# An earlier, two-part position bias and strictly alternating partial matmuls in the first block of a two-block kernel

## The chip, the cores and the metric

One Trainium2 chip, one NeuronCore of it. The metric is the device time of one execution, in microseconds (us). The kernel before was timed three times: 1125.5, 1128.43 and 1130.07 us, so its median is 1128.43 us. A further execution was profiled; its own time is 1129.25 us.

## The reference

Two transformer blocks run one after the other on a sequence of 256 tokens of width 1024, all in float32. The change lies in the first one, whose mixer has two attention branches of eight heads each and needs this, cut to what matters here:

```python
h = rmsnorm(x, norm_mix); proj = h @ w_in        # split into q_a, k_a, ..., kv_b, g_b, g_br
# branch A: an index scores every key, the best 64 of them are attended to
score = sum_h wi * relu(qi_h @ k_i.T)            # 8 index heads of width 32, causal
logits = q_a @ k_a.T * scale + table_a[t5_bucket(t - s)]
# branch B: compressed blocks, selected blocks, window; all three use the other 8 columns of the table
kc_cmp = compress_blocks(kc)                     # gelu(blk @ w1) @ w2 on blocks of 32 tokens, stride 16
logit_c = q_b @ kc_cmp.T * scale + table_b[t5_bucket(t - cmp_end)]
logit_s = q_b @ k_s.T * scale + table_b[t5_bucket(t - s)]
logit_w = q_b @ k_w.T * scale + table_b[t5_bucket(t - s)]
x = x + (sigmoid(gate_a) * (o_a @ w_branch_a) + sigmoid(gate_b) * (o_b @ w_branch_b)) @ w_out
```

The bias depends on the distance t - s alone: a table of 32 buckets by 16 heads (`rel_bias`) gives one value for each head and distance.

## The kernel before, in words

All weights stream from memory in units of 128 x 1024 float32 values (512 KB, two K-tiles of 512 columns). SyncE's queue issues the loads into four `raw` buffers (line 246); ScalarE rounds a unit to `hi` (line 262) and VectorE subtracts to get `lo` (line 263), each into four buffers; TensorE multiplies hi and lo with the hi and lo parts of the activations, three matmuls for each product (lines 349, 351, 352 where the result has features on partitions, 305 to 307 where it has tokens there). A raw buffer is free again when `lo` is made, so the stream runs a fixed number of units ahead of TensorE.

Small work is woven into these matrix products: `later` puts functions into a list, and each K-tile of a product takes one from it. Within this, a scheduler with a model of its own sets the order of TensorE's, VectorE's and ScalarE's queues; GpSimd's (POOL) and SyncE's queues keep the order in which the program is written. Every engine works its queue strictly in order.

In `block1_mix` the order of the products is: the token-wise columns (chunk 4 of `w_in`), queries and keys of the index (chunk 0), keys and values (chunk 1), `qb` (chunk 3), `qa` (chunk 2), then four chunks of gates, into which the attention itself is woven. What the change touches:

- `bias_job` (line 587). A matmul of `rb` with a one-hot matrix (line 590) gives the bias of 16 heads for 384 distances; VectorE adds the causal mask (`tv`, 592); GpSimd writes it sixteen times, once for each row of a group of 16 queries, to device memory (`tvd`, 595) and reads it back shifted by one element from row to row in eight DMAs (597), 16 queries with 16 heads each, into `BT` (128 x 16 heads x 256). Then GpSimd clears `cmpB` and copies every sixteenth column of heads 8 to 15 into it (600 to 602). The job is queued ahead of chunk 3.
- The memsets of `kcT`, `VB`, `gek`, `gev` (741, 743, 773), which stand behind that job in GpSimd's queue.
- The loads of the compression weights `w1k`, `w1v` (1 MB each, 703) and of `csk`, `csv`, and the copies of keys and values `kpk`, `kpv` (717, 718) from which `blkk`, `blkv` are added up (725).
- `index` (657): eight score matmuls for each 128 queries; each uses 32 rows of the 128 x 128 array (`32*128`), four such row groups in turn. `cmp1` (746): 16 matmuls into four column groups. `qk` (845): query-key products of the attention; each uses 64 rows, head pairs lie in the lower and the upper half. In the source these loops alternate between the groups already; the scheduler may place them in another order.
- `bm` (837, GpSimd) adds the index's mask to heads 0 to 7 of `BT` for branch A; the softmax (866) of branch B reads heads 8 to 15. The order of branches is selected, window, A.

Of the kernel before, what the change touches and what calls it, by code (L numbers as in the profile page):

```python
# [9 lines left out]
F32 = mybir.dt.float32  # L10
# [13 lines left out]
NEG = -1.0e30  # L24
# [185 lines left out]
class Prog:  # L210
# [343 lines left out]
    def block1_mix(self, x0, x):  # L554
        tc, nc, ap, g = self.tc, self.nc, self.ap, self.g
        with ExitStack() as es, ExitStack() as rs_:
# [3 lines left out]
            cp = pool("b1c", 1)  # L560
# [19 lines left out]
            BT = cp.tile([128, 16, 256], F32, name="BT")  # L580
# [7 lines left out]
            def bias_job():  # L588
# [37 lines left out]
            def small_done(t, ps):  # L626
                nc.scalar.activation(tms[:, t, :], ps, AF.Copy, scale=r0[:, t:t + 1])
                if t:
                    nc.scalar.activation(gb, tms[:, :, 328:352], AF.Tanh, scale=0.5)
                    nc.gpsimd.tensor_scalar(gb, gb, 0.5, 0.5, op0=ALU.mult, op1=ALU.add)  # L630
                    nc.gpsimd.dma_start(caus, ap["c1"][:, tot - 256:])
                    nc.gpsimd.dma_start(rest, ap["c1"][0:32, 128:896])
                    nc.gpsimd.dma_start(rb, ap["rel_bias"])
            stats()
# [16 lines left out]
            self.gemm_feat(W_IN1, 0, *xT, d0)  # L651

# [4 lines left out]
            def index(t, hps):  # L657
# [3 lines left out]
                for a in range(2):  # L661
                    for hp, ps in zip(hps, pss):
                        pr = slice(32 * hp, 32 * hp + 32)
                        nc.tensor.matmul(ps[:, a, :n], qi[pr, a, t * 128:t * 128 + 128], ki[pr, :n], start=True,
                                         stop=True)
# [35 lines left out]
            for nm in "kv":  # L701
                w1 = mp.tile([128, 16, 128], F32, name="w1" + nm)
                nc.gpsimd.dma_start(w1, ap["cmp_w1_" + nm])
                cs = mp.tile([128, 80], F32, name="cs" + nm)
                nc.gpsimd.dma_start(cs, ap["cmp_s_" + nm])
                cw.append((w1, cs))
            blks = []

            def d1(i, ps):
                nc.vector.tensor_tensor(kv[:, 2 * i:2 * i + 2, :], ps, bc2, op=ALU.mult)  # L710
                if i:
                    return
                for i, nm in enumerate("kv"):
# [5 lines left out]

                    blk = mp.tile([128, 16, 32], F32, name="blk" + nm)  # L720
                    nc.gpsimd.memset(blk[:, :, 30:32], 0.0)
                    for gr in range(2):
                        v = bass.AP(tensor=kp.tensor, offset=kp.offset + 256 * gr,
                                    ap=[list(kp.ap[0]), [2, 16], [16, 15]])
                        nc.gpsimd.tensor_tensor(blk[:, :, 15 * gr:15 * gr + 15], v,
                                                cw[i][1][:, 0:16].unsqueeze(2).to_broadcast([128, 16, 15]),
                                                op=ALU.add)
                    blks.append(blk)
# [7 lines left out]
            self.later(bias_job)  # L736
# [3 lines left out]
            kcT = cp.tile([128, 2, 16], F32, name="kcT")  # L740
            nc.gpsimd.memset(kcT, 0.0)
            VB = cp.tile([128, 2, 4, 64], F32, name="VB")
            nc.gpsimd.memset(VB, 0.0)
            cps = {}

            def cmp1(i):
# [3 lines left out]
                for l4 in range(4):  # L750
                    for q in range(4):
                        l = 4 * l4 + q
                        nc.tensor.matmul(ps[32 * q:32 * q + 32, :128], blks[i][:, l, :], cw[i][0][:, l, :],
# [882 lines left out]
```

## Time and profile before

| | |
|---|---|
| time, median of three runs | 1128.43 us (1125.5 to 1130.07) |
| the profiled execution's own time | 1129.25 us |
| its span, first to last instruction | 1127.5 us |
| TensorE busy | 1104.7 us, 98% of the span |
| VectorE, ScalarE, GpSimd busy | 762.8, 573.7, 93.3 us |
| mean granted TensorE clock | 0.993 of full speed |
| `block1_mix` | about the first 220 us |

A share of 98% says that nearly all of the time is TensorE's queue at work, so a change counts only by what it does to that queue: an instruction in it that becomes shorter, or a wait in it that goes or comes. Idle time of the other engines is read only for what it makes TensorE wait for.

### The profile page before, as it was taken

The page shows a single profiled execution, that of the slowest core. Times are in us where ns is not written, and L with a number is a line of the kernel's source. Part 1 is how long each engine was busy: PE and PEld are TensorE (multiplying, and loading weights), DVE is VectorE, ACT ScalarE, POOL GpSimd, SP SyncE. Part 2 cuts the span into 40 slices and gives each one's busy share as a digit, 9 for nine tenths or more (in the row PEclk, how much of TensorE's full clock was granted, in tenths as well). Part 3 has the DMA queues.
Part 4 walks back from the last instruction along what each step waited for, and adds up shares of the span by engine and source line. Part 5 has one row for each costly group of instructions (what it writes and reads, how often), then busy time and mean ns, then how long its engine had stood idle before and what let it go on. Part 6 is the DMA issues. An engine that isn't in the chain of part 4 may idle for free.

```text
span 1127.5 us, 17685 instructions
## 1 busy us (share of the span) xinstructions
PE 1104.7 (98%) x6852; PEld 986.4 (87%) x6852; DVE 762.8 (68%) x1230; ACT 573.7 (51%) x858; POOL 93.3 (8%) x135
## 2 busy tenths in 40 slices
PE   9998999999999999999999999999999999999997
PEld 8887899888888878888879999889999978888886
DVE  6766777677755567777458675556778777777643
ACT  6325544555544456555445336545555455655542
POOL 1411230000001010000001010001323000000000
PEclk9998999999999999999999999999999998999999
DMA  8794124655555646555556655444544565555552
GB/s 298 250 175 145 39 86 149 210 179 196 189 187 182 199 168 201 186 187 186 186 169 201 195 168 200 152 130 139 181 150 157 163 204 167 188 186 185 189 173 92
DMA packets 55908, 196.91 MB, mean 175 GB/s; under 512 B 6716, under 2 KB 6988, under 8 KB 55568
## 3 DMA queue, kind: packets, MB, share of 16 engines
q1 hardware_dynamic: 52704, 186.44, 50.2%
q0 software_dynamic: 2832, 9.21, 3.5%
q8 instruction: 54, 0.88, 0.3%
q14 instruction: 30, 0.25, 0.1%
q10 hardware_dynamic: 288, 0.14, 0.1%
HBM read 192.84 MB, written 1.44 MB: 172 GB/s over the span
## 4 chain that ended last, share of the span: by engine, by line
PE 92%; DVE 3%; DMA 3%; ACT 1%; issue 1%; POOL 0%; DVEq 0%; POOLq 0%; ACTq 0%
PE acc L368 20%; PE acc L369 10%; PE acc L305 10%; PE acc L306 9%; PE acc L307 9%; PE acc L351 8%; PE acc L349 8%; PE acc L352 8%; DMA BT<-tvd 2%; PE sm L854 2%; PE o L893 1%; DVE lo L263 1%; PE tr L880 1%; PE o L1437 1%; PE sm L1407 1%; PE tr L399 1%
## 5 line engine op out<-in xcount | busy, mean ns | idle before, releaser
L263 DVE TENSOR_TENSOR lo<-raw,hi 128x1024 fp32r<-128x1024 f32 (+2 forms) x356 | 433.3, 1219 | 264.8 <-ACT hi L262 262.4
L262 ACT ACTIVATE hi<-raw 128x1024 fp32r<-128x1024 f32 (+2 forms) x356 | 371.2, 1044 | 425.4 <-issue 120.9
L368 PE MATMUL acc<-xs,hi 128*128 128x512 f32 x960 | 340.4, 400 | 1.3 <-DVE sum L374 1.0
L369 PE MATMUL acc<-xs,lo 128*128 128x256 f32 x960 | 268.8, 281 | 0.0
L368 PEld LDWEIGHTS acc<-xs,hi 128*128 128x128 f32 x960 | 180.8, 189 | 44.8 <-DVE sum L374 1.4
L349 PE MATMUL acc<-xs,hi 128*128 128x256 f32 (+1 forms) x696 | 198.7, 288 | 0.3 <-ACT hi L262 0.3
L351 PE MATMUL acc<-xs,hi 128*128 128x256 f32 (+1 forms) x696 | 198.1, 286 | 0.0
L352 PE MATMUL acc<-xs,lo 128*128 128x256 f32 (+1 forms) x696 | 197.0, 286 | 0.1
L369 PEld LDWEIGHTS acc<-xs,lo 128*128 128x128 f32 x960 | 181.9, 189 | 0.5
L349 PEld LDWEIGHTS acc<-xs,hi 128*128 128x128 f32 (+1 forms) x696 | 132.9, 192 | 3.4 <-issue 2.4
L351 PEld LDWEIGHTS acc<-xs,hi 128*128 128x128 f32 (+1 forms) x696 | 133.5, 192 | 1.9 <-issue 1.5
L352 PEld LDWEIGHTS acc<-xs,lo 128*128 128x128 f32 (+1 forms) x696 | 132.8, 192 | 1.6 <-issue 1.0
L305 PE MATMUL acc<-hi,hT 128*128 128x512 f32 x304 | 117.9, 390 | 1.0 <-DVE x L1069 1.0
L306 PE MATMUL acc<-lo,hT 128*128 128x512 f32 x304 | 118.5, 390 | 0.0
L307 PE MATMUL acc<-hi,hT 128*128 128x512 f32 x304 | 118.0, 389 | 0.0
L305 PEld LDWEIGHTS acc<-hi,hT 128*128 128x128 f32 x304 | 57.1, 188 | 13.3 <-DVE x L1069 1.5
L307 PEld LDWEIGHTS acc<-hi,hT 128*128 128x128 f32 x304 | 57.1, 188 | 12.0
L306 PEld LDWEIGHTS acc<-lo,hT 128*128 128x128 f32 x304 | 57.1, 188 | 11.5
L305 PE MATMUL acc<-hi,xs 128*128 128x386 f32 (+1 forms) x128 | 47.7, 375 | 1.6 <-DVE f L1160 1.5
L306 PE MATMUL acc<-lo,xs 128*128 128x386 f32 (+1 forms) x128 | 48.0, 375 | 0.0
L307 PE MATMUL acc<-hi,xs 128*128 128x386 f32 (+1 forms) x128 | 46.8, 370 | 0.0
L374 DVE TENSOR_TENSOR sum<-acc,sum 128x512 f32<-128x512 f32 x60 | 41.0, 684 | 0.0
(430 smaller groups left out, 1344.5 us busy)
## 6 DMA issues: line engine op xcount, KB each, us to landing
raw<-in_w_in SPq DMA_DIRECT2D x100, 512.0 KB, 3.5
raw<-in_ffn_w_gate SPq DMA_DIRECT2D x44, 512.0 KB, 3.5
raw<-in_ffn_w_up SPq DMA_DIRECT2D x44, 512.0 KB, 3.4
raw<-in_ffn_w_down SPq DMA_DIRECT2D x44, 512.0 KB, 3.4
raw<-in_w_mlp_in SPq DMA_DIRECT2D x32, 512.0 KB, 3.4
raw<-in_w_mlp_out SPq DMA_DIRECT2D x32, 512.0 KB, 3.2
raw<-in_w_out SPq DMA_DIRECT2D x16, 512.0 KB, 3.5
raw<-in_w_in SPq DMA_DIRECT2D x16, 386.0 KB, 3.1
```

Of the source, the lines that this page charges most:

```text
L262: nc.scalar.activation(hi[:, :n * w], raw[:, :n * w], AF.Copy)
L263: nc.vector.tensor_tensor(lo[:, :n * w], raw[:, :n * w], hi[:, :n * w], op=ALU.subtract)
L305: nc.tensor.matmul(ps[t][:, :w], xh[:, k, sl], hi, start=(k == 0), stop=False)
L306: nc.tensor.matmul(ps[t][:, :w], xh[:, k, sl], lo, start=False, stop=False)
L307: self.last_mm = nc.tensor.matmul(ps[t][:, :w], xl[:, k, sl], hi, start=False, stop=last)
L349: nc.tensor.matmul(o, hi[:, fs], xh[:, k, :], start=(k == 0 and f % 2 == 0), stop=False, skip_group_check=True)
L351: nc.tensor.matmul(o, hi[:, fs], xl[:, k, :], start=False, stop=False, skip_group_check=True)
L352: nc.tensor.matmul(o, lo[:, fs], xh[:, k, :], start=False, stop=last, skip_group_check=True)
L368: nc.tensor.matmul(ps[:, f, :, :], hi[:, fs], x.both[:, k, :, :], start=(k == 0), stop=False)
L369: nc.tensor.matmul(ps[:, f, 0, :], lo[:, fs], x.hi[:, k, :], start=False, stop=last)
L374: nc.vector.tensor_tensor(s, ps[:, :, 0, :], s, op=ALU.add)
L854: nc.tensor.matmul(ps[:, i, :], q[pr:pr + 64, U["fts"][i], t * 128:t * 128 + 128], kk, start=True, stop=True)
```

## The change

`bias_job` becomes two parts. `bias_table` (matmul, mask, write to memory) is called right behind chunk 0. `bias_rows(g)` reads back eight heads in eight DMAs; it is called with g = 1 (heads 8 to 15) ahead of chunk 1 and with g = 0 behind the first chunk of gates. `BT` becomes two tiles. The memsets stand ahead of the reads, the loads of `w1k`, `csk`, `csv` behind them; `w1v` is loaded behind the copies for `kpk` and `kpv`. The copies into `cmpB` follow `blkv`. `rest` and `rb` are loaded ahead of `caus`. A new helper, `in_turn`, forces each matmul of `index`, `cmp1` and `qk` behind the one written before it in TensorE's queue; it adds no instruction.

```diff
+    def in_turn(self, fs):
+        last = None
+        for f in fs:
+            with ExitStack() as es:
+                if last is not None:
+                    es.enter_context(self.tc.issue_after(last.ins))
+                last = f()
...
-            BT = cp.tile([128, 16, 256], F32, name="BT")
+            BT = [cp.tile([128, 8, 256], F32, name="BT%d" % g) for g in range(2)]
...
-            def bias_job():
+            def bias_table():
                 ps = self.psm()
                 nc.tensor.matmul(ps[:16, :384], rb, onehot, start=True, stop=True)
                 tv = bp.tile([16, 384], F32, name="tv")
                 nc.vector.tensor_tensor(tv, ps[:16, :384], neg, op=ALU.add)
-                tvd = self.dp.tile([16, 16, 384], F32, name="tvd")
+                tvd = box["tvd"] = self.dp.tile([16, 16, 384], F32, name="tvd")
                 nc.gpsimd.dma_start(tvd.rearrange("c h u -> h c u"), tv.unsqueeze(1).to_broadcast([16, 16, 384]))
+
+            def bias_rows(g):
+                tvd = box["tvd"]
                 for i in range(8):
-                    nc.gpsimd.dma_start(BT[16 * i:16 * i + 16, :, :],
-                                        bass.AP(tensor=tvd.tensor, offset=tvd.offset + 127 - 16 * i,
-                                                ap=[[16 * 384 - 1, 16], [384, 16], [1, 256]]))
-                nc.gpsimd.memset(cmpB, NEG)
-                nc.gpsimd.tensor_copy(cmpB[:, 1, :, 0:15], BT[:, 8:16, 31:256:16])
-                nc.gpsimd.tensor_copy(cmpB[:, 0, :, 0:7], BT[:, 8:16, 159:256:16])
+                    nc.gpsimd.dma_start(BT[g][16 * i:16 * i + 16, :, :],
+                                        bass.AP(tensor=tvd.tensor, offset=tvd.offset + 8 * 384 * g + 127 - 16 * i,
+                                                ap=[[16 * 384 - 1, 16], [384, 8], [1, 256]]))
...
             self.gemm_feat(W_IN1, 0, *xT, d0)
+            bias_table()
...
-                for a in range(2):
-                    for hp, ps in zip(hps, pss):
...
+                self.in_turn([lambda a=a, z=z: score(a, *z) for a in range(2) for z in zip(hps, pss)])
...
+            for tl in [kcT, VB] + ges + [b[:, :, 30:32] for b in blks]:
+                nc.gpsimd.memset(tl, 0.0)
+            nc.gpsimd.memset(cmpB, NEG)
+            bias_rows(1)
+            nc.gpsimd.dma_start(cw[0][0], ap["cmp_w1_k"])
+            for i, nm in enumerate("kv"):
+                nc.gpsimd.dma_start(cw[i][1], ap["cmp_s_" + nm])
...
+                nc.gpsimd.dma_start(cw[1][0], ap["cmp_w1_v"])
...
+                nc.gpsimd.tensor_copy(cmpB[:, 1, :, 0:15], BT[1][:, :, 31:256:16])
+                nc.gpsimd.tensor_copy(cmpB[:, 0, :, 0:7], BT[1][:, :, 159:256:16])
             self.gemm_feat(W_IN1, 1, *xT, d1)
...
-            self.later(bias_job)
             self.gemm_feat(W_IN1, 3, *xT, dq(qb))
...
+                self.in_turn([lambda l4=l4, q=q: part(l4, q) for l4 in range(4) for q in range(4)])
...
+                self.in_turn([lambda i=i, z=z: head(i, *z) for i in range(duo[0]["nh"]) for z in zip(duo, pss)])
...
             for c in range(4):
                 self.gemm_feat(W_IN1, 5 + c, *xT, gdone(c))
+                if c == 0:
+                    bias_rows(0)
```

What this does to the queues is seen at three places. First, GpSimd's queue between the bias and the gates. Before (gek, gev, kcT, VB are tiles of the compression; L601 and L602 read what the eight BT DMAs bring):

```order
L595 DMA tvd<-tv 16x16x384
L597 DMA BT<-tvd 16x16x256 x8
L600 MEMSET cmpB 128x256
L601 COPY cmpB<-BT 128x8x15
L602 COPY cmpB<-BT 128x8x7
L741 MEMSET kcT 128x32
L743 MEMSET VB 128x512
L773 MEMSET gek 128x32
L773 MEMSET gev 128x32
```

and with the change, where BT_175 is the tile of heads 8 to 15:

```order
L606 DMA tvd<-tv 16x16x384
L713 COPY fold<-ident 32x32 x4
L722 MEMSET kcT 128x32
L722 MEMSET VB 128x512
L722 MEMSET gek 128x32
L722 MEMSET gev 128x32
L722 MEMSET blkk 128x16x2
L722 MEMSET blkv 128x16x2
L723 MEMSET cmpB 128x256
L612 DMA BT_175<-tvd 16x8x256 x8
L725 DMA w1k<-in_cmp_w_k 128x2048
```

The memsets of gek and gev stand ahead of the reads of the bias instead of behind the copies that need them. The load of w1k now stands behind eight of these reads, where before it was issued ahead of the whole bias; csk, csv, the eight copies for kpk and kpv, and w1v follow it in this order, and the reads of heads 0 to 7 come only behind the first two gates.

Second, TensorE's queue at the first query-key products of branch A (sm<-ka,qa; acc rows are the gate product). Before:

```order
L854 MATMUL sm<-ka,qa 128x256 x2
L349 MATMUL acc<-xs,hi 128x256
L351 MATMUL acc<-xs,hi 128x256
L352 MATMUL acc<-xs,lo 128x256
L349 MATMUL acc<-xs,hi 128x256
L854 MATMUL sm<-ka,qa 128x256 x2
L351 MATMUL acc<-xs,hi 128x256
L352 MATMUL acc<-xs,lo 128x256
```

and with the change:

```order
L352 MATMUL acc<-xs,lo 128x256
L909 MATMUL o<-tms,PT 128x64 x8
L896 MATMUL tr<-ident,L 128x128 x8
L869 MATMUL sm<-ka,qa 128x256 x4
L349 MATMUL acc<-xs,hi 128x256
L351 MATMUL acc<-xs,hi 128x256
```

Two pieces of two matmuls become one of four, in the order lower, upper, lower, upper half. At the other places the forced order leaves one matmul alone and the other three (or seven) together some rows later: with the change the index runs in pieces of 1, 3, 1, 3 (256 columns) and 1, 3, 4 (128 columns), where before all eight pieces were of 2; the query-key products run in pieces of 1, 3, 1, 3 and 1, 7 for each of the first two branches and of 4, 4 and 1, 6, 1 for branch A.

Third, TensorE's queue at the compression (blkk, w1k: keys; blkv, w1v: values), with the change:

```order
L770 MATMUL sm<-w1k,blkk 32x128 x16
L349 MATMUL acc<-xs,hi 128x256
L351 MATMUL acc<-xs,hi 128x256
L352 MATMUL acc<-xs,lo 128x256
L349 MATMUL acc<-xs,hi 128x256
L351 MATMUL acc<-xs,hi 128x256
L352 MATMUL acc<-xs,lo 128x256
L349 MATMUL acc<-xs,hi 128x256
L351 MATMUL acc<-xs,hi 128x256
L352 MATMUL acc<-xs,lo 128x256
L349 MATMUL acc<-xs,hi 128x256
L770 MATMUL sm<-w1v,blkv 32x128 x16
```

Counted from row 129 of the queue, up to which both kernels are alike, 259 matmuls of the streamed products stand ahead of the keys' piece, before 187; ahead of the values' piece 269, before 220.

## Rows read from the trace of the kernel before

**Rows 1.** Busy time of each engine in stretches of 20 us: stretch, its length, for each engine busy us (and instructions), then granted TensorE clock, busy share of the DMA engines, GB/s.

```profile
80.00:100.00 20.00, 14.18 (x112) 12.70 (x111) 10.39 (x25) 9.28 (x21) 3.74 (x9) 0.83 0.67 194
100.00:120.00 20.00, 20.00 (x141) 17.55 (x140) 13.51 (x49) 8.89 (x32) 0.45 (x1) 1.00 0.18 56
120.00:140.00 20.00, 20.00 (x143) 16.97 (x141) 15.57 (x62) 11.02 (x41) 6.71 (x6) 1.00 0.15 52
```

**Rows 2.** The waits between 60 and 100 us: engine and line, what it waited for, us in total, times, longest.

```profile
POOL cmpB L601 <- DMA BT<-tvd: 19.7, 1, 19.7
ACT hi L262 <- DMA raw<-in_w_in: 11.9, 3, 6.4
...
PE sm L783 <- DVE gek L774: 5.8, 1, 5.8
...
DVE gek L774 <- POOL gek L773: 5.3, 1, 5.3
```

**Rows 3.** GpSimd's instructions in order of time: start, duration, instruction, idle time before it and what ended it.

```profile
27.00 0.53 POOL L632 DMA_DIRECT2D rest<-in_c  x1
...
34.83 0.54 POOL L703 DMA_DIRECT2D w1v<-in_cmp_w_v  x1
...
50.32 1.45 POOL L725 TENSOR_TENSOR blkv<-kpv,csv 128x240 f32<-128x240 f32 x2 [0.90 <-DMA kpv<-kv]
56.52 0.60 POOL L595 DMA_DIRECT2D tvd<-tv  x1 [4.76 <-DVE sc L686]
62.37 4.48 POOL L597 DMA_DIRECT2D BT<-tvd  x8 [5.24 <-DMA tvd<-tv]
...
86.89 0.37 POOL L601 COPY cmpB<-BT 128x120 f32<-128x120 f32 x1 [19.72 <-DMA BT<-tvd]
```

**Rows 4.** TensorE around its wait, in order of time, same columns.

```profile
81.05 0.28 PE L352 MATMUL acc<-xs,lo 128*128 128x256 f32 x1
...
82.25 0.28 PE L349 MATMUL acc<-xs,hi 128*128 128x256 f32 x1
88.34 0.40 PE L783 MATMUL sm<-gek,csk 128*64 128x16 f32 x4 [5.82 <-DVE gek L774]
88.68 0.63 PE L790 MATMUL sm<-csv,gev 128*16 128x64 f32 x16
...
89.62 0.42 PE L352 MATMUL acc<-xs,lo 128*128 128x256 f32 x1
...
91.33 0.35 PE L351 MATMUL acc<-xs,hi 128*128 128x256 f32 x1
```

**Rows 5.** One stretch behind that wait, columns as in group 1.

```profile
88.00:92.00 4.00, 3.65 (x35) 3.42 (x36) 2.73 (x5) 3.02 (x11) 0.58 (x3) 0.57 0.49 184
```

**Rows 6.** The chain of waits through the first 260 us. First its shares by line (of 260 us), then pieces of it: start, duration, engine, tile and line, number of records (each of these float32 matmuls leaves two).

```profile
by line: PE acc L351 12.0%; PE acc L349 11.9%; PE acc L352 11.8%; PE acc L368 9.2%; DMA BT<-tvd 7.8%; PE sm L854 6.6%; PE o L893 6.2%; PE acc L369 4.6%; PE tr L880 3.3%; PE acc L305 2.8%; PE acc L307 2.8%; PE acc L306 2.8%; PE sm L664 2.6%;
...
33.35 1.06 PE sm L664 x4
34.41 0.31 PE acc L349
...
43.59 0.64 PE sm L664 x4
...
96.32 1.06 PE sm L854 x4
...
123.81 0.63 PE sm L854 x2
...
143.46 1.06 PE sm L854 x8
...
150.20 0.42 PE sm L854 x2
...
152.55 1.08 PE sm L854 x14
```

**Rows 7.** TensorE's compression and bias matmuls in order of time, columns as in group 3.

```profile
54.83 0.81 PE L590 MATMUL sm<-rest,rb 32*16 32x384 f32 x2
...
59.35 1.08 PE L753 MATMUL sm<-w1k,blkk 128*32 128x128 f32 x32
...
64.51 1.08 PE L753 MATMUL sm<-w1v,blkv 128*32 128x128 f32 x32
```

**Rows 8.** The DMA queues between 62 and 87 us (packets, MB, share of the 16 engines' time) and the transfers issued there (count, KB each, median us from issue to landing).

```profile
q0 software_dynamic: 640, 2.10, 55.5%
q1 hardware_dynamic: 779, 2.85, 45.8%
...
raw<-in_w_in SPq DMA_DIRECT2D x5, 512.0 KB, 15.3
BT<-tvd POOLq DMA_DIRECT2D x8, 256.0 KB, 13.2
```

**Rows 9.** The same for the whole first 140 us: some of the transfers.

```profile
w1v<-in_cmp_w_v POOLq DMA_DIRECT2D x1, 1024.0 KB, 8.9
tvd<-tv POOLq DMA_DIRECT2D x1, 384.0 KB, 5.6
...
rest<-in_c POOLq DMA_DIRECT2D x1, 96.0 KB, 4.8
```

**Rows 10.** VectorE's waits between 96 and 156 us, columns as in group 2.

```profile
DVE L L866 <- PE sm L854: 9.6, 9, 2.2
```

More of the change, by code (lines that the diff above doesn't have):

```diff
@@ L660, in index, with score @@
                 pss = [self.psm().rearrange("p (a b) -> p a b", a=2) for _ in hps]
-                for a in range(2):
-                    for hp, ps in zip(hps, pss):
-                        pr = slice(32 * hp, 32 * hp + 32)
-                        nc.tensor.matmul(ps[:, a, :n], qi[pr, a, t * 128:t * 128 + 128], ki[pr, :n], start=True,
-                                         stop=True)
+                def score(a, hp, ps):
+                    pr = slice(32 * hp, 32 * hp + 32)
+                    return nc.tensor.matmul(ps[:, a, :n], qi[pr, a, t * 128:t * 128 + 128], ki[pr, :n], start=True,
+                                            stop=True)
+                self.in_turn([lambda a=a, z=z: score(a, *z) for a in range(2) for z in zip(hps, pss)])
                 for hp, ps in zip(hps, pss):
@@ L701, in block1_mix @@
             for nm in "kv":
[L702 to L707, printed above, removed]
+                cw.append((mp.tile([128, 16, 128], F32, name="w1" + nm), mp.tile([128, 80], F32, name="cs" + nm)))
+            blks = [mp.tile([128, 16, 32], F32, name="blk" + nm) for nm in "kv"]
+            kcT = cp.tile([128, 2, 16], F32, name="kcT")
+            VB = cp.tile([128, 2, 4, 64], F32, name="VB")
+            ges = [mp.tile([128, 2, 16], F32, name="ge" + nm) for nm in "kv"]
+            for tl in [kcT, VB] + ges + [b[:, :, 30:32] for b in blks]:
[5 more added lines that the diff above has]
+                nc.gpsimd.dma_start(cw[i][1], ap["cmp_s_" + nm])
             def d1(i, ps):
@@ L712, in d1 @@
                     return
+                kps = []
                 for i, nm in enumerate("kv"):
@@ L718, in d1 @@
                         nc.gpsimd.dma_start(kp[64:128, gr, 0:255], src[:, 1:256])
-                    blk = mp.tile([128, 16, 32], F32, name="blk" + nm)
-                    nc.gpsimd.memset(blk[:, :, 30:32], 0.0)
+                    kps.append(kp)
+                nc.gpsimd.dma_start(cw[1][0], ap["cmp_w1_v"])
+                for i, kp in enumerate(kps):
                     for gr in range(2):
@@ L749, in cmp1, with part @@
                 ps = self.psm()
[L750 to L753, printed above, removed]
-                                         start=(l4 == 0), stop=(l4 == 3), skip_group_check=True)
+                def part(l4, q):
+                    l = 4 * l4 + q
+                    return nc.tensor.matmul(ps[32 * q:32 * q + 32, :128], blks[i][:, l, :], cw[i][0][:, l, :],
+                                            start=(l4 == 0), stop=(l4 == 3), skip_group_check=True)
+                self.in_turn([lambda l4=l4, q=q: part(l4, q) for l4 in range(4) for q in range(4)])
                 hq = mp.tile([128, 128], F32, name="hq" + nm)
@@ L771, in cmp1b @@
                 nc.scalar.activation(th, u, AF.Tanh, scale=0.7978845608028654)
-                ge = mp.tile([128, 2, 16], F32, name="ge" + nm)
-                nc.gpsimd.memset(ge, 0.0)
+                ge = ges[i]
                 nc.vector.scalar_tensor_tensor(ge[:, :, 0:15], th.rearrange("p (a b) -> p a b", a=2), 1.0,
@@ L847, in qk, with head @@
                 pss = [self.psm().rearrange("p (a b) -> p a b", a=duo[0]["nh"]) for _ in duo]
-                for i in range(duo[0]["nh"]):
-                    for U, ps in zip(duo, pss):
-                        br, t, pr = U["br"], U["t"], U["pr"]
-                        n = 128 * (t + 1)
-                        q = qa if br == 0 else qb
-                        kk = ka[pr:pr + 64, :n] if br == 0 else kv[pr:pr + 64, 1 + br, :n]
-                        nc.tensor.matmul(ps[:, i, :], q[pr:pr + 64, U["fts"][i], t * 128:t * 128 + 128], kk,
-                                         start=True, stop=True)
+                def head(i, U, ps):
+                    br, t, pr = U["br"], U["t"], U["pr"]
+                    n = 128 * (t + 1)
+                    q = qa if br == 0 else qb
+                    kk = ka[pr:pr + 64, :n] if br == 0 else kv[pr:pr + 64, 1 + br, :n]
+                    return nc.tensor.matmul(ps[:, i, :], q[pr:pr + 64, U["fts"][i], t * 128:t * 128 + 128], kk,
+                                            start=True, stop=True)
+                self.in_turn([lambda i=i, z=z: head(i, *z) for i in range(duo[0]["nh"]) for z in zip(duo, pss)])
                 for U, ps in zip(duo, pss):
@@ L864, in softmax @@
                 for i, h in enumerate(U["heads"]):
-                    b = U["bm"][:, i, :] if br == 0 else BT[:, 8 + h, j0:j0 + n]
+                    b = U["bm"][:, i, :] if br == 0 else BT[1][:, h, j0:j0 + n]
                     nc.vector.tensor_tensor_reduce(L[:, i, :], ps[:, i, :], b, op0=ALU.add, op1=ALU.max, scale=1.0,
```

13 lines of the change are left out of this document (4 added, 9 removed).

## The prediction

> **What bounds the kernel now.** I read the time of each engine by stretches first. TensorE is busy without a gap in the stretches of the first block except one: between 80 and 100 us it works 14.18 of 20 us, and its granted clock is 0.83 there and 1.00 next to it [rows 1]. Next come the waits around that stretch: one wait of TensorE, 5.8 us at line 783, for VectorE's `gek`; VectorE waited 5.3 us for GpSimd's memset of `gek`; GpSimd waited 19.7 us for the DMAs into `BT` [rows 2]. So a memset that needs nothing stands in GpSimd's queue behind copies that need the last of 2 MB. GpSimd's instructions in order of time show the chain's start: the bias is written out at 56.52, the reads go out at 62.37, and the copy starts at 86.89 [rows 3]. Everywhere else TensorE's own instructions are the time, so the second thing to read is what the small matmuls cost in its queue: the chain of waits gives line 854 (query-key) 6.6% and line 664 (index) 2.6% of 260 us, 17.2 and 6.8 us [rows 6].
>
> **The change, part by part.** *The memsets.* With the change they stand ahead of everything that waits, so line 783's successor waits for VectorE's own chain alone, which was itself held by the memset [rows 2]. What goes is 5.82 us of idle time [rows 4]. Behind it TensorE ran slowly: the same 256-column matmuls come every 0.21 us between 89.62 and 91.33 (eight steps), against 0.12 us between 81.05 and 82.25 (ten) [rows 4], with a granted clock of 0.57 in that stretch [rows 5]: the 1.2 GHz level, after the idle time. The eight steps lose 0.75 us, and the two small pieces ahead of them (0.4 and 0.55 us) about half their length: 1.2 us. Together 7.0 us.
>
> *Query-key products.* A piece of two matmuls of 256 columns took 1.06 us, one alone 0.63, so each further one costs 0.43; but a piece of eight records, four matmuls, also took 1.06, and one of fourteen records (seven of 128 columns) 1.08, where one alone took 0.42 [rows 6]. That is what it looks like when neighbours use different halves of the array and run side by side, and when they don't. With strict alternation every adjacent pair does. Pieces of 1 and 3 cost 0.63 + 1.06, pieces of 1 and 7 0.42 + 1.08. The first two branches cost 2 x (0.63 + 1.06) + 1.50 = 4.88 us each, branch A 2 x 1.06 + 0.42 + 0.86 + 0.42 = 3.82 (0.86: three slots of 0.22 and the 0.2 that any piece adds). Sum 13.6 against 17.2: 3.6 us less.
>
> *Index.* Its pieces of two, all in one row group, cost 1.06 and 0.64 [rows 6], four of each, 6.8 us. Pieces of 1, 3, 1, 3 and 1, 3, 4 cost 2 x (0.63 + 1.06) + 0.42 + 0.64 + 0.64 = 5.1, if groups of 32 rows overlap as halves do: 1.7 us less. That overlap isn't in the trace; if there is none, it is 0.2 us less. The nearest row, sixteen matmuls in four groups of 32 columns in 1.08 us [rows 7], speaks for the overlap. I take 1.7.
>
> *Interruptions.* The first matmul of a product behind a small piece takes 0.31 us instead of 0.12 [rows 6]; TensorE's queue has 45 such places where it had 43: 0.4 us more. The matmuls of `cmp1` overlapped already (1.08 us for sixteen [rows 7]): nothing.
>
> *The bias matmul* moves from 54.83 [rows 7] to just ahead of the first index matmul, which stood at 33.35 [rows 6] and is now five product matmuls (0.6 us) later, so to 34 us, and waits in TensorE's queue for `rest`, `rb`. `rest` was issued at 27.00 [rows 3] and took 4.8 us [rows 9], so it is there by 31.8, 2 us early, and is now issued first of its group: nothing. VectorE waits for it with the next weight units behind, in time in which it was idle for the index's first scores; nothing.
>
> *The DMAs.* `tvd` went out 1.7 us after the bias matmul's start (54.83 to 56.52 [rows 7, 3]), so now near 35.7; it takes 5.6 us [rows 9], and the eight half-size reads go out from 41 us. 2 MB of reads cost 55.5% of 25 us of all 16 engines, 13.9 us [rows 8]; half of it is 7 us, and 12 to 13 at the share they get beside the weights. So heads 8 to 15 land near 54, w1k behind them near 59 (w1v took 8.9 us [rows 9] behind a load of its own size, so about half for each), kpk and kpv near 61, and w1v, issued near 61 and taking 5 to 9 us, near 66 to 70. TensorE needs w1k and w1v where? The keys' piece stood at 59.35 [rows 7] with 187 product matmuls ahead and has 259 now: 72 x 0.12 = 8.6 us later, less 1.5 for the shorter index: 66. The values' piece follows at 68. So w1k is there by some 7 us, w1v just so. The cost is 0 if it lands by 68, and up to 4 if a little over the worst case; I take 0.5. Next in line behind that are `cmpB` (GpSimd near 66, needed near 76) and heads 0 to 7: 1 MB, 4.5 us of issue in GpSimd's queue as for the whole bias [rows 3], behind the first gates, when DMA is busy at 0.18 and 0.15 [rows 1] and the first reader is 30 us away: nothing. Were that cover gone, branch A's bias would be late by the same 10 us.
>
> *Waits that the faster queue brings.* VectorE and ScalarE get their scores sooner and TensorE their results not. Nothing of it is in the trace; bounds 0 and the 3.6 us gained. VectorE waited for these products nine times, 9.6 us in all, and not the other way round [rows 10]: nearer 0; I take 0.5.
>
> The sum: -5.8 - 1.2 - 3.6 - 1.7 + 0.4 + 0.5 + 0.5 = -10.9 us. What follows the first block is TensorE's queue, so all of it reaches the end. From the profiled execution's 1129.25 that gives 1118.3; it lay 0.8 above the median, so **1117.5 us** against 1128.43.
>
> **The rivals.** *Softmax takes the place of the products.* VectorE and ScalarE must empty both halves before the next pair may start, so TensorE's gain there comes back as waits. For it: VectorE is busy 13.5 and 15.6 of 20 us there [rows 1]. Against it: [rows 10]. The sum without the 3.6 and with the index at its low bound: 1117.5 + 3.6 + 1.5 = 1122.6, at most. The Trainium skill ("TensorEngine Tiling (Array Packing)", Performance Considerations, PSUM Bottleneck) says it so: packing speeds up TensorE but not the emptying of PSUM, which may become the bottleneck. By that page the gain of 3.6 us would be gone.
>
> *The weights or w1v are a little late.* The early reads share the engines with the weight stream: with the bias in flight a unit took 15.3 us to land [rows 8], and ScalarE waited 11.9 us for weights [rows 2], which TensorE's wait covered. Without that cover, and with w1k and w1v in the same stretch, TensorE idles 3 to 6 us and perhaps loses its clock once more (1.2): 1121 to 1124, middle 1122.5. Against it: the buffers hold some four units of 24 matmuls, 11.5 us. The skill ("DMA: Bandwidth & Descriptors", Issuing engines are not separate DMA queues) bears on this: all transfers run on the same 16 engines and interleave, whoever issues them. The 15.3 us agree.
>
> *Slower: the half-size reads take as long as the whole ones.* Then heads 8 to 15 land 24 us after 41, at 65, as they did from 62.37 to 86.89 [rows 3]. w1k, queued behind, lands near 70, `blkk` is ready at 73: TensorE waits 7 us at the keys' piece (66). w1v follows at 77 to 81, 3 to 6 us after TensorE wants it: 11 to 13 in all, and twice 1.2 for the clock. From 1117.5, less 0.5 counted already, that is 1130 to 1132. It decides for slower once w1v is some 11 us late, at 79. Against it: the bytes and rows are half.
>
> *The pairs don't run side by side or the order does not hold.* Then the first part alone stands: 1117.5 + 3.6 + 1.7 = 1122.8. The order of the queue and [rows 6] speak against it.
>
> **How the numbers follow.** Forecast 0.62; softmax 0.13; weights or w1v late 0.14; slower 0.07; no overlap 0.04. A measurement of this kernel can tell about 0.5%, 5.6 us, from no change: 1122.8. The forecast's own case reaches from 1113.5 (no new wait, and the 2.9 us by which the fastest run lay under the median) to 1121. The range takes in most of the first two rivals: 1113.5 to 1123.5; left out are the slower case and the tails. Faster by over 0.5%: 0.62 x 0.97 and about 0.6 of 0.31, 0.79; slower 0.06; the rest, 0.15, within.
>
> **What would show it.** TensorE without a wait at the successor of line 783 and a clock of 1.00 from 60 to 100 us; the chain's share of the query-key line near 13.6 us and of the index line near 5.1; reads of heads 8 to 15 landed by 55, w1v by 68. Wrong it would be if TensorE waits at the `cmp1` pieces for `w1v` or `blkv`, if ScalarE's waits for weights become TensorE's, or if TensorE's transposes wait for ScalarE's exponentials.

## The result, and the profile after

The changed kernel took 1114.89 us, median of four runs, against 1129.25 us for the kernel before in the same set (a fourth run of 1136.72 us has joined the three): ratio 0.9873, 95% interval 0.9852 to 0.9894. In a second set, further down, it was 1116.73 against 1127.17 us, ratio 0.9904 (0.9891 to 0.9917). Forecast were 1117.5 us, in a range of 1113.5 to 1123.5. The profiled execution took 1113.66 us, its span was 1111.9 us.

The busy time in the stretches around the old wait, columns as in [rows 1]:

```profile
60.00:80.00 20.00, 19.52 (x222) 18.42 (x221) 15.91 (x47) 8.89 (x18) 6.88 (x9) 1.00 0.67 225
80.00:100.00 20.00, 20.00 (x155) 17.62 (x155) 14.86 (x58) 9.88 (x27) 5.47 (x10) 1.00 0.64 156
```

Between 80 and 100 us TensorE no longer stands still and its clock is 1.00, where it was busy for 14.18 us at 0.83 [rows 1]. All that TensorE still waits for between 20 and 190 us is one transfer:

```profile
PE sm L770 <- DMA w1v<-in_cmp_w_v: 0.5, 1, 0.5
```

That is the wait which the prediction had entered with 0.5 us. The chain of waits through the first 260 us, its shares by line and then pieces of it (start, duration, line, records), answers [rows 6]:

```profile
by line: PE acc L368 12.7%; PE acc L351 11.5%; PE acc L349 11.5%; PE acc L352 11.2%; PE acc L369 6.3%; PE o L909 6.0%; PE sm L869 5.2%; DMA w1k<-in_cmp_w_k 4.5%; PE tr L896 3.2%; DMA w1v<-in_cmp_w_v 2.8%; PE acc L307 2.8%; PE acc L305 2.8%;
...
81.77 0.63 PE sm L869 x2
84.85 1.06 PE sm L869 x6
...
94.30 0.41 PE sm L869 x2
95.38 1.09 PE sm L869 x14
```

The query-key line (854 before, 869 now) has 5.2% of 260 us, 13.5 us, where it had 17.2. One matmul of 256 columns takes 0.63 us and the three behind it 1.06, one of 128 columns 0.41 and seven 1.09: these are the pieces that the sum was made of. The index's matmuls in TensorE's order of time (start, duration, instruction):

```profile
33.47 0.69 PE L677 MATMUL sm<-ki,qi 32*128 32x256 f32 x2
36.91 1.12 PE L677 MATMUL sm<-ki,qi 32*128 32x256 f32 x6
...
46.80 0.71 PE L677 MATMUL sm<-ki,qi 32*128 32x128 f32 x6
50.25 0.71 PE L677 MATMUL sm<-ki,qi 32*128 32x128 f32 x8
```

In the same view of the kernel before, each line is one piece of two matmuls:

```profile
36.44 1.13 PE L664 MATMUL sm<-ki,qi 32*128 32x256 f32 x4
...
43.52 0.71 PE L664 MATMUL sm<-ki,qi 32*128 32x128 f32 x4
```

Three matmuls of 256 columns now take what two took, and three or four of 128 columns take what two took: groups of 32 rows run side by side, which no row of before had shown. GpSimd in order of time answers [rows 3]:

```profile
34.41 0.59 POOL L606 DMA_DIRECT2D tvd<-tv  x1 [2.72 <-DVE tv L604]
...
40.61 4.20 POOL L612 DMA_DIRECT2D BT<-tvd  x8 [3.39 <-DMA tvd<-tv]
46.56 0.57 POOL L725 DMA_DIRECT2D w1k<-in_cmp_w_k  x1 [1.75 <-DMA BT<-tvd]
...
58.64 0.52 POOL L739 DMA_DIRECT2D kpv<-kv  x1 [5.04 <-DMA w1k<-in_cmp_w_k]
...
60.17 0.56 POOL L741 DMA_DIRECT2D w1v<-in_cmp_w_v  x1
...
65.96 1.38 POOL L749 COPY cmpB<-BT 128x120 f32<-128x120 f32 x1
```

The bias goes out at 34.41 instead of 56.52 us, and `cmpB` is copied at 65.96 without a wait, where it was at 86.89 after 19.72 us of waiting.

**A measure that the start-up and the end don't blur.** For the experiments I count on TensorE from the start of its first transposes of `rt` (line 549 before, 558 after) to its first matmul at line 305 with `mT`, behind the gates: "the stretch". Within it I add, from TensorE's instructions in order of time, the time from each row's start to the next row's start, by what the row computes. It took 171.12 us before and 158.75 after: 12.4 us of the change's 15.6 us of span lie there. The rest is the start-up (28.31 against 27.15 us until the stretch begins) and what lies behind it (928.1 against 926.0), where both kernels have the same instructions in the same order.

Each run without "twice" has one trace, so its stretch is one execution. The medians of the table stand beside 1127.2 to 1128.3 us for the kernel before in the same sets.

| run | stretch | index | query-key | TensorE's waits over 0.3 us | median us, ratio to before (95%) |
|---|---|---|---|---|---|
| before, twice | 171.1, 169.8 | 6.8 | 17.3 | `gek` 5.8, 3.6 | |
| the change, twice | 158.8, 159.4 | 5.1 | 13.6 | `w1v` 0.5, 1.1 | 1116.7, 0.9904 (0.9891 to 0.9917) |
| memsets alone | 164.9 | 6.8 | 14.1 | `Lc` 3.1 | 1122.3, 0.9955 (0.9937 to 0.9973) |
| alternation alone | 169.5 | 5.1 | 14.8 | `gek` 7.5 | 1125.5, 0.9970 (0.9947 to 0.9992) |
| memsets and alternation, bias late | 165.8 | 5.1 | 13.7 | `Lc` 6.5 | 1122.8, 0.9964 (0.9950 to 0.9977) |
| bias part alone, twice | 162.2, 162.2 | 6.8 | 15.7 | none | 1117.6, 0.9909 (0.9886 to 0.9931) |
| whole bias early | 166.5 | 5.0 | 14.8 | `w1v` 3.6 | 1121.6, 0.9951 (0.9932 to 0.9970) |
| w1k first | 161.7 | 5.1 | 13.6 | `w1v` 1.9 | 1117.0, 0.9903 (0.9890 to 0.9917) |
| both weights first | 162.8 | 5.1 | 14.2 | `blkv` 1.5, `blkk` 0.9 | 1120.0, 0.9937 (0.9922 to 0.9952) |
| both weights from SyncE | 164.3 | 5.1 | 14.2 | `hi` 2.4, `lo` 0.8 | 1120.7, 0.9933 (0.9919 to 0.9948) |

### The profile page after: what moved, and what is told of

Read it like the earlier page. It is cut to its first block, busy times and chain, and to the rows that moved or that the text cites. A ratio compares the mean times of both kernels' runs of the same rounds, so it can differ in the third digit from the quotient of the medians.

```text
span 1111.9 us, 17700 instructions
## 1 busy us (share of the span) xinstructions
PE 1094.0 (98%) x6852; PEld 978.1 (88%) x6852; DVE 760.2 (68%) x1230; ACT 574.0 (52%) x858; POOL 95.9 (9%) x143
## 4 chain that ended last, share of the span: by engine, by line
PE 93%; DMA 3%; DVE 2%; ACT 1%; issue 0%; POOL 0%; DVEq 0%; SPq 0%; ACTq 0%; POOLq 0%
PE acc L368 20%; PE acc L369 10%; PE acc L305 10%; PE acc L306 10%; PE acc L307 10%; PE acc L349 8%; PE acc L351 8%; PE acc L352 8%; PE o L909 1%; PE sm L869 1%; DMA w1k<-in_cmp_w_k 1%; PE tr L896 1%; PE o L1455 1%; PE sm L1425 1%; PE tr L399 1%; DMA w1v<-in_cmp_w_v 1%
```

## The experiments

### The memsets alone

```diff
@@ block1_mix, kernel before; cut @@
             blks = []
+            kcT = cp.tile([128, 2, 16], F32, name="kcT")
+            VB = cp.tile([128, 2, 4, 64], F32, name="VB")
+            ges = [mp.tile([128, 2, 16], F32, name="ge" + nm) for nm in "kv"]
+            for tl in [kcT, VB] + ges:
+                nc.gpsimd.memset(tl, 0.0)
...
-            nc.gpsimd.memset(kcT, 0.0)
...
-            nc.gpsimd.memset(VB, 0.0)
...
-                nc.gpsimd.memset(ge, 0.0)
```

> The kernel before, with one edit: the four memsets of kcT, VB, gek and gev stand ahead of everything in GpSimd's queue that waits; the bias is still built late and read whole. The theory of the forecast: TensorE's wait of 5.8 us goes, and with it the 1.2 us lost to the low clock behind it, 7.0 us in all, since the wait was for a memset and not for the bias; VectorE's sum of the compressed scores needs cmpB only near 88 us, when the copies are done. Median about 1122, clock 1.00 in the stretch from 80 to 100 us. The rival: the late bias itself was the limit, so that the wait moves on to the compressed scores (which need cmpB) or to the first window softmax (which needs heads 8 to 15 at 87 us), and 3 us or less are gained.

Measured: ratio 0.9955, about 5 us less; 6.2 us less in the stretch than in the first trace of before, 5.6 less than in the mean of its two. The wait for `gek` is gone, but another has come. First VectorE's wait, for its sum `Lc` of compressed scores and `cmpB`, and TensorE's, then GpSimd's copy, then the stretch from 80 to 100 us:

```profile
DVE Lc L918 <- POOL cmpB L602: 4.0, 1, 4.0
...
PE sm L854 <- DVE Lc L918: 3.1, 1, 3.1
```

```profile
84.33 0.38 POOL L601 COPY cmpB<-BT 128x120 f32<-128x120 f32 x1 [18.21 <-DMA BT<-tvd]
```

```profile
80.00:100.00 20.00, 16.91 (x109) 14.82 (x109) 14.16 (x51) 8.88 (x23) 2.29 (x5) 0.91 0.49 151
```

The rival is right in this: with TensorE no longer held by the memset, the late bias was next, through `cmpB`. My theory's "7.0 us from the memsets" was wrong; only part of it comes from them. The query-key products also became shorter (17.3 to 14.1 us) without any forced order: in the order that the scheduler gave this kernel they lie in 14 pieces, where they lay in 18.

### The alternation alone

```diff
@@ index; the same in cmp1 and qk, kernel before @@
-                for a in range(2):
-                    for hp, ps in zip(hps, pss):
-                        ...
+                self.in_turn([lambda a=a, z=z: score(a, *z) for a in range(2) for z in zip(hps, pss)])
```

> The kernel before, with one edit: the strict alternation of the index, query-key and cmp1 matmuls; the memsets and the bias stay where they were. The theory: the index and query-key pieces shorten by 5.3 us, less 0.4 for places where the products are interrupted and 0.5 for new waits, so 4.4 us are gained, while the wait of 5 to 6 us for gek and the low clock behind it stay. Query-key line 13.6 us of TensorE's queue where it was 17.2, index line 5.1 where it was 6.8. The rival (softmax takes the place of the products): the lines shorten, but TensorE's transposes wait for ScalarE, and the gain is 1 us or less. The other rival (no overlap): the lines keep their time and nothing is gained.

Measured: ratio 0.9970; 1.6 us less in the stretch than in the first trace of before, 0.9 less than in the mean of its two, not 4.4. The lines did shorten, by 1.7 and 2.5 us, and TensorE has no wait but the old one, so neither rival holds. But that wait grew from 5.8 us (3.6 in the second trace) to 7.5:

```profile
PE sm L794 <- DVE gek L785: 7.5, 1, 7.5
```

```profile
80.00:100.00 20.00, 12.54 (x95) 11.13 (x94) 8.89 (x19) 7.65 (x17) 3.45 (x9) 0.74 0.61 176
```

The reason is in GpSimd's order of time: the bias is written out no sooner than before, though its table `tv` is ready sooner. First `tv`, on VectorE, then GpSimd:

```profile
53.22 0.53 DVE L601 TENSOR_TENSOR tv<-sm,rest 16x384 f32<-16x384 f32 x1
```

```profile
54.00 1.74 POOL L735 TENSOR_TENSOR blkv<-kpv,csv 128x240 f32<-128x240 f32 x1 [0.46 <-DMA kpv<-kv]
55.68 0.60 POOL L604 DMA_DIRECT2D tvd<-tv  x1
...
87.02 0.38 POOL L610 COPY cmpB<-BT 128x120 f32<-128x120 f32 x1 [20.61 <-DMA BT<-tvd]
```

Counted from the first transposes, `tvd` goes out after 28.2 us in the kernel before (56.52 - 28.31) and 28.3 us here (55.68 - 27.36). The two dates are alike, but not for one reason. Before, GpSimd was through with `blkv` after 23.5 us and stood 4.76 us for VectorE [rows 3], whose `tv` was done after 27.9 us: the bias matmul, behind the index, set the date. Here `tv` is done 1.5 us sooner, after 26.4 us, but GpSimd finishes `blkv` only after 28.4. The alternation thus moved the limit from `tv` to `blkv`; why GpSimd came later isn't shown (its waits for the copies of keys and values, and the additions themselves, were longer). The reads behind it also took longer, 31.3 us from `tvd`'s issue to the copy of `cmpB` against 30.4 and 28.2 in the two traces of before. What TensorE saves ahead of its wait it spends in it.

### Both, with the bias late

> The kernel before, with the early memsets and the strict alternation together; the bias is still built late and read whole. The memsets alone left TensorE waiting 3.1 us at the query-key line for the sum of the compressed scores with cmpB. The theory: the time at which the bias's copy goes out is set by GpSimd's queue (behind blkv) and not by the index, so what the alternation saves ahead of that wait (1.7 us of index, and the first query-key pieces) is waited out there: a wait of about 4.8 us, and about 163 us from the first transposes to the first matmul of the mixer, against 164.9 for the memsets alone and 158.8 for the changed kernel. So the alternation is worth some 2 us here and 3.4 us behind the early bias. The rival (the parts add up, whatever the bias does): 164.9 - 3.4 = 161.5 us, and a wait of 3.1 us as with the memsets alone.

The edit is the two diffs above together. Measured: ratio 0.9964 and 165.8 us. The index and query-key lines are short (5.1 and 13.7 us), and TensorE waits for the compressed scores longer than in any other kernel:

```profile
PE sm L865 <- DVE Lc L930: 6.5, 1, 6.5
```

With the bias late, the alternation gained nothing on top of the memsets (165.8 against 164.9 us in the stretch). `tvd` went out 28.2 us after the first transposes in both: with the memsets alone it waited for `tv` (27.9), here for `blkv` (28.3), as in the experiment above. Of the 3.4 us by which the wait grew, some 1.7 are the shorter index; the other 1.7 are slower reads: from `tvd`'s issue to the copy of `cmpB` it took 30.5 us here and 28.9 with the memsets alone. The two traces of before differ by 2.2 us in this, so it may be scatter; but both traces with the alternation and a late bias have the longer times (30.5 and 31.3), so that the alternation slows the reads isn't ruled out. Without these 1.7 us it would be near 164.1 us, still 2.6 above the 161.5 of the rival. So the parts don't add up: in these traces the alternation pays only once nothing late stands behind it.

### The bias part alone

```diff
@@ in_turn, changed kernel @@
-                    es.enter_context(self.tc.issue_after(last.ins))
+                    pass
```

> The changed kernel without the strict alternation: the bias part alone (memsets early, bias early, in halves, weights ordered anew). The theory: 7.0 us under the kernel before, as for the memsets alone, because the early bias adds nothing that the memsets did not give, and 4 to 5 us over the changed kernel. The rival: the early bias gives something of its own (the compressed scores or the softmax no longer wait), then it is over 8 us under the kernel before.

> The bias part alone once more, for a second trace. If its stretch of 162.2 us was typical, it comes within 0.5 us again, without a wait at the cmp1 pieces, and the alternation is worth the difference to the changed kernel's 158.8 and 159.4 us, some 3 us; if it comes near 159.5, the alternation is worth little behind the early bias.

Measured: ratio 0.9909; the stretch 162.2 us in both traces, 8.2 us under the mean of the two traces of before, and TensorE does not wait at all in it. So the rival was right and the theory wrong:

```profile
60.00:80.00 20.00, 20.00 (x226) 18.94 (x226) 16.29 (x49) 7.97 (x15) 6.07 (x7) 1.00 0.64 216
80.00:100.00 20.00, 20.00 (x143) 17.38 (x142) 14.35 (x52) 9.90 (x29) 6.03 (x10) 1.00 0.62 150
```

So the early bias gives 2.7 us that the memsets don't (162.2 against 164.9). That is a net figure: the products, with the wait in them, take 5.0 us less (112.1 to 107.1), but in this kernel's order the query-key pieces take 1.6 us more (14.1 to 15.7), and the output products and transposes 0.8. Behind the early bias the alternation gives 2.8 to 3.4 us. In the times this last step cannot be seen: 1117.6 in one set, 1116.7 for the change in another. The traces show it: 1.7 us in the index and 2.2 in the query-key line, of which the products, interrupted more often, and the wait for `w1v` take some back.

### The whole bias early

```diff
@@ block1_mix, changed kernel @@
             bias_rows(1)
+            bias_rows(0)
             nc.gpsimd.dma_start(cw[0][0], ap["cmp_w1_k"])
...
                 self.gemm_feat(W_IN1, 5 + c, *xT, gdone(c))
-                if c == 0:
-                    bias_rows(0)
```

> The changed kernel with one edit: heads 0 to 7 are read right behind heads 8 to 15, ahead of w1k, so the whole 2 MB of bias are read early. The theory: the reads of 2 MB take 24 us as before, from 41 to about 65 us; w1k lands between 70 and 75, w1v near 85, and TensorE, which wants the values' weights near 77 in the order of this kernel, waits 5 to 9 us there and loses clock behind it: 6 to 10 us over the changed kernel. The rival: the reads are hidden, or the weights go out beside them, and the time is that of the changed kernel within 1.5 us: then reading eight heads at a time is worth nothing.

Measured: ratio 0.9951; 7.4 us more in the stretch than the mean of the change's two traces, within the 6 to 10 of the theory, though the wait itself is 3.6 us and not 5 to 9. TensorE's wait, GpSimd's issues, and two stretches of 20 us:

```profile
PE sm L771 <- DMA w1v<-in_cmp_w_v: 3.6, 1, 3.6
```

```profile
67.90 0.52 POOL L740 DMA_DIRECT2D kpv<-kv  x1 [3.24 <-DMA w1k<-in_cmp_w_k]
...
69.77 0.56 POOL L742 DMA_DIRECT2D w1v<-in_cmp_w_v  x1
```

```profile
60.00:80.00 20.00, 16.23 (x165) 15.52 (x167) 13.53 (x32) 6.36 (x6) 9.78 (x15) 0.95 1.02 344
80.00:100.00 20.00, 20.00 (x176) 18.85 (x169) 10.20 (x24) 7.80 (x19) 1.71 (x2) 0.88 0.32 102
```

`w1v` is issued 9.6 us later than in the change (69.77 against 60.17). Of the 7.4 us 2.8 are a longer wait, 1.2 longer query-key pieces in this kernel's order; the rest lies behind the wait, where the clock is 0.95 and 0.88 in the two stretches. That is what reading eight heads at a time is worth, by one trace.

### The weights earlier

Three edits try to remove the wait of 0.5 us for `w1v` that the change brought.

```diff
@@ w1k first @@
-            bias_rows(1)
             nc.gpsimd.dma_start(cw[0][0], ap["cmp_w1_k"])
             ...
+            bias_rows(1)
@@ both weights first: w1v as well, ahead of bias_rows(1) @@
@@ both weights from SyncE: in d1, in place of the two loads above @@
+                nc.sync.dma_start(cw[0][0], ap["cmp_w1_k"])
+                nc.sync.dma_start(cw[1][0], ap["cmp_w1_v"])
```

> The changed kernel with one edit: w1k and the two small loads beside it are issued ahead of the reads of heads 8 to 15, not behind them. The order of TensorE's queue is the same. In the changed kernel GpSimd stood 5.0 us before a copy for kpv until w1k had landed, and w1v, behind it, came 0.5 us late. The theory: w1k lands near 50 us, that stand of GpSimd shortens to 1 us or less, w1v is issued some 4 us sooner and lands by 64 us, the wait of 0.5 us goes, and heads 8 to 15 land by 60 us where nobody waits for them (cmpB is read near 76): 0.5 us less in the stretch of the block, too little for the time to tell. The rival (GpSimd then stands for the last reads of the bias just as long): w1v keeps its 60.2 us of issue and the wait stays.

> The changed kernel with w1k, w1v and the two small loads all issued ahead of the reads of heads 8 to 15. TensorE's queue changes a little in the scheduler's hands. The theory: both weights land by 55 us, no wait for them is left; 2 MB of weights stand ahead of 1 MB of reads, which land near 62 us, in time for cmpB (read near 76 us): within 1.5 us of the changed kernel's 158.8 us for the stretch. The rival: 3 MB at once delay the stream of weights, ScalarE gets its units late, and TensorE waits 2 us or more between 45 and 65 us.

> The changed kernel with w1k and w1v issued by SyncE, in the stream of weight units, instead of GpSimd. In all traces so far each of GpSimd's DMA issues stood until the one eight places ahead of it had landed; w1k stood there between the bias's reads and the copies of kpv, and w1v behind both. The theory: without the two large loads in that queue no issue of it waits for w1k, the copies for kpv go out by 55 us and blkv is ready by 62 us, w1v is issued near 50 us and lands by 62 us, the wait at the cmp1 pieces (0.5 and 1.1 us in two runs of the change, with 1.9 us and a drop of the clock in one with w1k first) goes: 157.5 to 159 us for the stretch of the block, and a time at or up to 1.5 us under that of the changed kernel. The rival: 2 MB ahead of the next weight units in SyncE's queue delay those, ScalarE splits them late, and TensorE waits 1 to 4 us for hi or lo between 50 and 75 us.

Measured: 161.7, 162.8 and 164.3 us for the stretch; none is shorter than the change's 158.8 and 159.4, and all three theories fell; with `w1k` first and with SyncE the rivals were right, with both first neither was (the time with w1k first, 1117.0 us, can't be told from the change's). With w1k first, GpSimd only stands (issues nothing, until an earlier transfer has landed) elsewhere, among the reads:

```profile
47.33 1.64 POOL L612 DMA_DIRECT2D BT<-tvd  x3 [4.01 <-DMA w1k<-in_cmp_w_k]
...
60.68 0.57 POOL L741 DMA_DIRECT2D w1v<-in_cmp_w_v  x1
```

`w1v` is issued at 60.68 instead of 60.17 us; TensorE waits 1.89 us and then runs the values' piece at half speed, as its order of time shows:

```profile
69.16 1.90 PE L770 MATMUL sm<-w1v,blkv 128*32 128x128 f32 x32 [1.89 <-DMA w1v<-in_cmp_w_v]
```

With both first, the copies of keys and values are pushed back (the last goes out at 60.56 us instead of 59.66), and TensorE waits 1.5 us for `blkv` and 0.9 for `blkk`; it waits for no weight unit. From SyncE, the 2 MB delay the weight stream, as the rival said; TensorE's waits, with ScalarE's and VectorE's parts of a unit at their head:

```profile
PE acc L349 <- ACT hi L262: 2.4, 1, 2.4
PE acc L352 <- DVE lo L263: 0.8, 1, 0.8
```

The Trainium skill ("DMA: Bandwidth & Descriptors", Issuing engines are not separate DMA queues) says that transfers of all engines run on the same 16 engines and interleave. The trace agrees: with SyncE as issuer the 16 engines were busy for 0.97 of the time between 40 and 70 us, in the change for 0.99, so the other queue brought no more of them. ScalarE waited 5.2 us for units between 40 and 80 us, where in the change it waited for none: the 2 MB now stand ahead of the units in SyncE's own queue. No order that I tried beats the one of the change.

### The change and the kernel before once more

> The changed kernel once more, beside the others of this call and of the kernel before on the same chip. If what its trace showed is the change and not a good run, the stretch from the first transposes to the first matmul of the mixer takes 158.8 us within 0.3, and the time is 12 to 14 us under the kernel before. If part of the 13.5 us of the first comparison was scatter of the run before (its start-up was 1.1 us longer and its products between 425 and 530 us ran 2 us slower), the medians lie nearer 12.4 apart.

> The kernel before once more, for a second trace. If the trace of before is typical, the stretch from the first transposes to the first matmul of the mixer takes 171.1 us within 0.5, with one wait of 5 to 6 us for gek; the start-up before it (28.3 us, against 26.8 to 27.4 in the others) and the rest behind it (928.1 us, against 923.7 to 929.0) may differ by 1 to 3 us, since they scatter in kernels that are the same there.

Measured: the change 159.4 us in the stretch, with 1.1 us of wait for `w1v`, and 10.4 us between the medians; the kernel before 169.8 us, with 3.6 us of wait for `gek`. TensorE's waits, the change first:

```profile
PE sm L770 <- DMA w1v<-in_cmp_w_v: 1.1, 1, 1.1
```

```profile
PE sm L783 <- DVE gek L774: 3.6, 1, 3.6
```

All of these lie outside what was expected, by 0.3 to 1.6 us. So the old wait scatters more than I had allowed: from `tvd`'s issue to the copy of `cmpB` it took 30.4 us in the first trace (86.89 - 56.52) and 28.2 in the second (84.18 - 56.01). Between the means of the two traces each, the change is worth 11.4 us in the stretch (170.4 against 159.1). What lies behind the stretch scatters by as much as the parts of the change: 928.1 and 926.1 us before, 926.0 and 925.5 after, 923.7 and 925.4 with the bias part alone.

## Why the prediction was right, point by point

- *The wait and the clock, 7.0 us.* Right as a sum for the trace it was made from: the products, waits included, took 114.5 us of the stretch before and 107.1 with the bias part alone, 7.4 less (6.1 less than in the second trace of before). The reason was incomplete: the prediction gave all of it to the memsets. The memsets alone leave a wait of 3.1 us and a clock of 0.91, and the early `cmpB` takes those away. That the change holds the early bias too, and the sum so came out, is luck as far as the reason goes. The prediction had looked at the new date of `cmpB` only for harm ("GpSimd near 66, needed near 76"), not for what the old date would have cost. The wait itself was 5.8 us in one execution and 3.6 in another.
- *Query-key, 3.6 us.* 3.7 us (17.3 to 13.6), all of it piece by piece as costed. But not all of it is the forced order: 1.5 us came with the bias part alone, in whose order the scheduler placed the pieces otherwise; 2.2 us are the alternation's.
- *Index, 1.7 us.* 1.7 us (6.8 to 5.1). The overlap of groups of 32 rows, assumed from the 32-column groups, is there.
- *Interruptions, 0.4 us.* Against the kernel before it can't be read, since the slow clock lies in the same products. Counted in TensorE's order of time, a product row follows another kind of row 50 times in the stretch with the change, 48 times before and 44 times with the bias part alone; the products without the wait took 0.6 us more than with the bias part alone (108.2 - 0.5 - 107.1), 0.1 us for each of six more places, where the prediction had 0.2.
- *The DMAs.* Of the dates, these held within 2 us: `tvd` 34.4 us (forecast 35.7), the last read, by GpSimd's stands, ahead of 53.1 (54), w1k 58.4 (59), w1v issued 60.2 (61) and landed 67.6 (66 to 70), keys' piece 64.75 (66). One did not: the copies for `kpv` landed between 62.0 and 65.2, not near 61, because three of the four stood behind `w1k`'s landing; `blkv` was ready at 66.0, 1.2 us before TensorE could use it. The wait for w1v was 0.5 and 1.1 us (0.5): by the prediction's own words a wait at this place was a sign of being wrong, and it came, at the size that the sum had entered.
- *Waits that the faster queue brings, 0.5 us.* Not there: TensorE waits for nothing else in the stretch. The Trainium skill ("TensorEngine Tiling (Array Packing)", Performance Considerations, PSUM Bottleneck) warns that emptying PSUM may become the bottleneck once TensorE is packed; here it did not: VectorE goes on waiting for these products (4.8 us between 80 and 142 us, from its waits), and TensorE never for VectorE.
- *Not in the sum.* The output products of the attention and the transposes between them took 0.6 us less (16.05 to 15.70, 7.39 to 7.13 us). That and the 0.5 above make most of the difference between 10.9 forecast and 12.4 us traced; against the mean of two traces it is 11.4.
- *From 1118.3 to the median.* Forecast were 10.9 us. The first set gave 14.4 us between the medians, the second 10.4. Some of the first is scatter outside the change: in the first trace of before the feed-forward products at line 368 took 399 ns each between 425 and 530 us, in the second 391, in the change 394 and 391.
- *The rivals.* Softmax: no. Weights late: by 0.5 to 1.1 us, not 3 to 6; the whole bias early shows that this rival was near, 7.4 us. Half-size reads as slow as whole ones: no, heads 8 to 15 were there 12.5 us after their first issue (40.61 to 53.1) instead of 24.5 us. No overlap: no.

## What to carry to other kernels

Before a stall is put down to the instruction that stands last in it, ask what the next consumer of the same late data would wait for: here taking away the memset alone moved the wait to `cmpB`, and a speed-up ahead of a wait whose date stayed where it was bought little or nothing until the date itself moved. When a date stays, ask whether it is still set by the same instruction: here it went from `tv` to `blkv` within 0.1 us. Shortening pieces in one engine's queue can be costed from single pieces of the trace, within 0.1 us here, but the parts of a change add up only where no wait lies behind them. Where the rest of a kernel scatters by more than the effect, compare a stretch between two instructions that both kernels have, from two traces of each.

## What the hardware showed that I had not expected

- **GpSimd's DMA issues stand for the one eight places ahead.** In none of the 13 traces does a DMA of GpSimd's queue start before the one eight places earlier has landed, and every stand within the first 100 us that no data explain ends 0.28 or 0.29 us behind that landing. In the change the second copy for `kpv` stands 5.04 us for `w1k` (landed at 58.35, issue at 58.64); with w1k first it is the sixth read of the bias (4.01 us); with both weights first the fifth read stands for `w1k` and the seventh for `w1v`:

```profile
45.04 1.05 POOL L612 DMA_DIRECT2D BT<-tvd  x2 [3.30 <-DMA w1k<-in_cmp_w_k]
50.02 1.05 POOL L612 DMA_DIRECT2D BT<-tvd  x2 [3.94 <-DMA w1v<-in_cmp_w_v]
```

  So a large load in that queue holds up the eighth issue behind it, whatever that one needs. Whether the chip or the program's semaphores set the eight wasn't tried.
- **A read of half the size is issued hardly faster.** Eight reads took 4.20 us of GpSimd's queue with 128 KB each and 4.48 us with 256 KB [rows 3]; from issue to landing they took 8.0 and 13.2 us [rows 8], median.
- **The clock after short idle time.** Behind waits of 0.47 and 1.09 us the values' piece took its usual 1.08 us; behind one of 1.89 us it took 1.90, and the clock was 0.91 between 60 and 80 us, where it was 1.00 in the two others. With both weights first two waits follow each other, and the second piece is slow behind 1.48 us:

```profile
64.57 1.08 PE L769 MATMUL sm<-w1k,blkk 128*32 128x128 f32 x32 [0.89 <-POOL blkk L745]
67.14 1.94 PE L769 MATMUL sm<-w1v,blkv 128*32 128x128 f32 x32 [1.48 <-POOL blkv L745]
```

  TensorE's order with w1k first is that of the change, so the stretches compare: 1.4 us more of wait than in the change's first trace made it 3.0 us longer, while 0.6 us more in the change's second trace made it 0.6 longer.
